# A seam as a planned list: the last block of a feed-forward layer and the first projections of the attention behind it

## The chip, the cores and the metric

The kernel runs on one core of a Trainium2 chip. The metric is the device time of one execution in microseconds, the median of the runs. The core's engines work side by side, each through its own queue of instructions in a fixed order: TensorE (PE, matrix products), VectorE (DVE), ScalarE (ACT), GpSimd (POOL) and SyncE (SP, which here issues the DMA transfers). An instruction starts when the one ahead of it on its engine and the instructions of other engines on which it depends are done.

## The reference, cut to what matters

Two layers on x of 1024 rows (S) by 1024 columns (D). Layer 0 mixes by a gated recurrence, layer 1 by stick-breaking attention with 16 heads of 64, and a SwiGLU feed-forward with an inner width of 2816 follows each. An RMS norm stands ahead of every sub-layer, a residual add behind it. The change lies at the seam between the feed-forward of layer 0 and the attention of layer 1:

```python
def swiglu_ffn(x, w_in, w_out):
    gu = jnp.einsum("bsd,df->bsf", x, w_in)
    h = jax.nn.silu(gu[..., :D_FF]) * gu[..., D_FF:]
    return jnp.einsum("bsf,fd->bsd", h, w_out)
...
    qkv = jnp.einsum("bsd,de->bse", x, w_qkv).reshape(bsz, seq, 3, N_HEADS, HEAD_DIM)
    ...
        z = jnp.einsum("bhqd,bhkd->bhqk", qb, kb).astype(jnp.float32) * scale
```

## The kernel before, in words

**Layout.** Activations lie transposed, columns on the 128 partitions: `h[d][n]` is part d (0 to 7) of the residual stream, half n (0 or 1, 512 rows). Every product is done in three passes (`mm3`, L545 to L547: high by high, low by high, high by low), so each operand exists as a rounded high part and the rest: for a part of the normed stream `xh` (ScalarE, L625) and `xl` (VectorE, L626), which the views name vh, vl or xg by the storage they use; for weights "hi" on ScalarE and "lo" on VectorE.

**The last block of the feed-forward.** The output product (p_ps) runs in 13 visits, each a pair of output parts d and d + 4 over a range of inner blocks. A visit makes seven products by combined weights instead of eight (`ORDER` is 0, 1, 2, 3, 4, 6, 5). Products that share a `BANK` add onto each other in PSUM; products 0, 2, 3 and 4 are first copied to SBUF by ScalarE (ta, tb; L1466) and products add to or subtract from `h` on VectorE ("post", L1468, L1470). A `Weights` object makes the combined weights: b (wbh, wbl), c (wch, wcl), d (wd). As soon as an `h[d][n]` is complete, `finished(d, n)` stores it (hd), makes xh and xl (`prep`) and adds its square to the sum of squares of half n (`squares`: ScalarE into acc, VectorE into rbc). In the generic loop this comes one product after the part was completed. The last visit, with parts 0 and 4, runs in this loop too, and a load and split of Q's first weights (raw, whi, wlo) is put between its products.

**The start of the attention.** A loop written out by hand takes the 8 parts (k = 0 to 7) of Q half 0, Q half 1, K half 0, K half 1 (qk_ps), and between them the steps of the row factors (`stats_steps`: sums L611, root, spread L592) and the splits of the next weights (`later`). Behind each group its result is scaled by the row factors (t, L1878), split (qh L1882, ql L1886), and SP moves it into per-head tiles (q, kh, kl; L1901; four moves for a half of Q, eight for a half of K). Loads of further weights (raw, L526) stand on the same queue, each where its group of the program calls for it.

**The plan.** All behind it is a `Plan`: tasks with an engine, an estimated cost, what they come after, and a rank. `emit` takes, again and again, the ready task that could begin first by these estimates (ties by rank), and writes it to its engine's queue. `attention_plan` holds the score chunks (z_ps, two banks in turn), their exponentials on ScalarE (F, L1953), the scans, the turned weights (wt_ps), the V products (av_ps) and the further projections.

Of the kernel before, what the change touches and what calls it, by code (L numbers as in the profile page):

```python
# [13 lines left out]
ALU = mybir.AluOpType  # L14
# [16 lines left out]
LATE = NB  # L31
FIRST = (ND, ND + 1, ND + 2, 0)


class Plan:
# [7 lines left out]
    def emit(self):  # L43
        end, free, table = {}, dict(self.free), {}
        todo, users = [], [[] for _ in self.tasks]
        for i, (_, _, _, after, _, _) in enumerate(self.tasks):
            after[:] = {a if isinstance(a, int) else a[0][a[1]] for a in after}
            todo.append(len(after))
            for a in after:
                users[a].append(i)  # L50
        ready = [i for i, n in enumerate(todo) if n == 0]
        while ready:
            best = None
            for i in ready:
                eng, us, _, after, rank, tab = self.tasks[i]
                begin = max([free[eng], *(end[a] + (0.0 if self.tasks[a][0] == eng else 0.15) for a in after)])
# [17 lines left out]
            fn()  # L74


# [113 lines left out]

def attention_plan(plan, fn):
    NP, LEAD = HEADS // 2, 8
# [24 lines left out]
    def weights(i, name, r, raw, use):  # L217
        ld = plan.add("dma", 4.8, fn["load", name], [raw], r - 4)
        h0 = plan.add("act", 0.5, fn["whi", name, 0], [ld, use], r - 2.5)
# [8 lines left out]
    is_kept = lambda q, n: q < NP - 2 + (n == 0)  # L228
    order = []
    for hx in range(2):  # L230
        moved[0, 1, 0, hx] = [plan.add(f"clock{hx}", 1.3 + 2.4 * hx, fn["wait", 0])]
    for i, (q, which, n) in enumerate(groups):
        s, wi = 24 * (q - 1) + 4 * (i % 6), 3 * q + which
        if i >= 4:
            if n == 0 and wi > 2:
                weights(wi, (q, which), s, wraw.get(wi - 3), wuse.get(wi - 2))
            p = None
            for k in range(ND):
                need = [p, pt.get(i - 2) if k == 0 else None]
                if wi > 2:  # L240
                    need.append(wlo[q, which][k // 4])
                p = plan.add("pe", 0.705, fn["proj", q, which, n, k], need, s + k / 2 + 0.5)
            proj[i] = wuse[wi] = p
        s += 4
        if i < 3:
            continue
        p = proj.get(i)
        if which < 2:
            order.append(i)
            was = order[-3] if len(order) > 2 else None  # L250
            pt[i] = plan.add("dve", 0.6, fn["t", q, which, n], [p, *moves.get(was, ())], s + 0.1)
            th = plan.add("act", 0.5, fn["qh", q, which, n], [pt[i], *moves.get(was, ())], s + 0.2)
# [7 lines left out]
        else:  # L260
            old = [(vadd, (q - 2, x)) for x in range(2)] if q > 1 else []
            pt[i] = plan.add("dve", 0.6, fn["t", q, which, n], [p, *old], s + 0.1)
            before = (dv, (q, n - 1) if n else (q - 1, 1)) if q or n else None
# [35 lines left out]
    tl, av, ring, banks, sums = {}, {}, [], [], {}  # L299
    stored = None  # L300
# [149 lines left out]
def trunk(  # L450
# [106 lines left out]
    class Mix:  # L557
# [8 lines left out]
        def load(self, i):  # L566
            self.raw[i] = load_raw(self.src[self.order[i]])
# [420 lines left out]
    def mix_out_ffn_in(h, mix, bias, layer, gnext, ob):  # L988
# [131 lines left out]
        with tc.manual_schedule(engines={E.PE, E.Activation, E.DVE, E.Pool}):  # L1120
# [359 lines left out]
            def finish(w):  # L1480
# [165 lines left out]
                end_plan(Plan(pe=0.0, act=0.9, dve=2.2, dma=0.0), Steps(acts), d0, d1, done).emit()  # L1646

            last_use = {p: max(u for u, (_, p0, p1) in enumerate(VISITS) if p0 <= p < p1) for p in range(NF // 2)}
            for s_, (kind, x) in enumerate(steps[:looped]):
# [18 lines left out]
                for k, i in enumerate(ORDER):  # L1668
# [4 lines left out]
                    part(banks[b], w, i, rhs[i], range(len(rhs[i])), onto=not new)  # L1673
                    if not final and kind == "v" and x == NV - 1:
                        if k == 0:
                            raw = load_raw(w_qkv[0])
                        elif k == 4:
                            qh = ring.four.tile([P, D], F32R, tag="w", name="whi")
                            nc.scalar.copy(qh, raw)
                        elif k == 5:  # L1680
                            ql = ring.four.tile([P, D], F32R, tag="w", name="wlo")
                            V.tensor_sub(ql, raw, f32(qh))
                            k3 = lambda t: t.rearrange("p (k c) -> p k c", k=ND)
                            wq0.append((k3(qh), k3(ql)))
                    if kind == "f":
                        post(x, i, banks[b])
                    else:
# [3 lines left out]
                        for dn in old:  # L1691
                            if final and x == NV - 3 and k >= L - 2:
# [90 lines left out]
            if not final:  # L1783
                for dn in done:
                    finished(*dn)
                del done[:]
        if final:
            with tc.manual_schedule(engines={E.PE, E.Activation, E.DVE, E.Pool, E.SP}):
                finish(nw)
        gs.close()  # L1790
# [7 lines left out]

    w_qkv, wq0 = attn_w_qkv, []
    mix_ffn(0, h, mix, V_BO, V_MIX + ND)  # L1800
# [16 lines left out]
    with ExitStack() as st:  # L1817
# [18 lines left out]
        TP, WH, WL, AV, OO, OH, OB = {}, {}, {}, {}, {}, {}, {}  # L1836
        W[0, 0] = wq0[0]

# [20 lines left out]

        def product(ps, name, k, n):  # L1860
            hi, lo = W[name] if name == (0, 0) else (k3(t) for t in W[name])
            mm3(ps, hi[:, k], lo[:, k], xh[k][n], xl[k][n], k == 0, k == ND - 1)

        def project(q, which, n, k):
            if k == 0:
                PS[q, which, n] = bank(psQ, "qk", n, "qk_ps")
            product(PS[q, which, n], (q, which), k, n)

# [186 lines left out]

        def stats_steps():
            for n in range(NH):
                stats(rbc[n], psO, f"o{n}", n)
                for _ in range(ND - (1 if n else 6)):
                    yield  # L2060
                broadcast_r(psO, f"o{n}", n)
                yield

        E = mybir.EngineType
        with tc.manual_schedule(engines={E.PE, E.Activation, E.DVE, E.Pool, E.SP}):
            sts, later = stats_steps(), []
            load((0, 1))
            load((0, 2))
            for i in range(4 * ND):
                if i >= 5:  # L2070
                    next(sts, None)
                g, k = divmod(i, ND)
                if k == 0:
                    if g:
                        was = (0, (g - 1) // 2, (g - 1) % 2)
                        scaled(*was)
                        q_hi(*was)
                        q_lo(*was)
                        for x in range(4 + 4 * was[1]):
                            move(*was, x)  # L2080
                    if g % 2 == 0:
                        name = (0, g // 2 + 1)
                        later += [
                            lambda a=name: w_hi(a, 0),
                            lambda a=name: (w_lo(a, 0), w_hi(a, 1)),
                            lambda a=name: w_lo(a, 1),
                        ]
                project(0, g // 2, g % 2, k)
                if i >= 5 and later:
                    later.pop(0)()  # L2090
# [64 lines left out]
```

## Time and profile before

| what | before |
|---|---|
| median of 3 runs | 2184.44 us (2180.5, 2184.44, 2184.8) |
| profiled execution, its own time | 2184.28 us |
| span of that execution | 2182.2 us |
| mean granted TensorE clock | 0.996 |
| TensorE busy | 2166.0 us (99%) |
| VectorE, ScalarE busy | 1705.2 us (78%), 1076.2 us (49%) |
| DMA | 274.62 MB, mean 126 GB/s |

Rows of a timeline give the start in microseconds from the span's start, the duration, the engine, the line, the operation, what it writes and reads and its shape, and in brackets the idle time of the engine just before with what ended it. TensorE's products overlap in part: what counts is the distance from one start to the next. Rows of the waits give the total, how often, and the longest. Rows of the windows give the stretch and its length, then the busy time of PE, PEld, DVE, ACT and POOL with their counts, then the granted clock of TensorE, the DMA share and GB/s.

### The profile page before, as it was taken

What the parts mean: (1) busy time and instruction counts of PE and PEld (TensorE: products, weight loads), DVE (VectorE), ACT (ScalarE), POOL (GpSimd) and SP (SyncE); (2) the same over time, 40 slices, a digit from 0 to 9 for tenths busy, and PEclk for the clock granted to TensorE, in tenths of its full rate; (3) what the DMA queues carried; (4) which work ended last, traced back from release to release, by engine and by line L of the source; (5) the groups of instructions that cost most, each with busy time, mean ns of one, the idle gap of its engine ahead of it and who ended that gap; (6) DMA issues with size and microseconds to landing.
All of it is one profiled execution on the core that took longest, in us unless ns stands there. A gap on an engine that the chain in (4) does not pass through costs nothing.

```text
span 2182.2 us, 27245 instructions
## 1 busy us (share of the span) xinstructions
PE 2166.0 (99%) x10066; PEld 1798.5 (82%) x10066; DVE 1705.2 (78%) x2431; ACT 1076.2 (49%) x1775; POOL 29.1 (1%) x38
## 2 busy tenths in 40 slices
PE   9999999999999999999999999999999999999998
PEld 7888888888888888877888888888888888888787
DVE  7978678677777887877888888877876777787887
ACT  5577445334444544644555555544543444454555
POOL 0000020000000000000000000001000000000000
PEclk9999999999999999999999999999999999999999
DMA  4111312244444854434333343442133444467452
GB/s 175 39 49 49 126 39 82 95 142 145 138 152 135 289 186 122 146 106 110 103 88 105 88 106 97 137 171 97 49 116 115 146 150 139 150 226 249 127 161 85
DMA packets 133317, 274.62 MB, mean 126 GB/s; under 512 B 15296, under 2 KB 23872, under 8 KB 133184
## 3 DMA queue, kind: packets, MB, share of 16 engines
q1 hardware_dynamic: 132768, 272.36, 39.5%
q8 instruction: 79, 1.29, 0.2%
q10 hardware_dynamic: 416, 0.52, 0.1%
q14 instruction: 54, 0.44, 0.1%
HBM read 176.88 MB, written 70.78 MB: 113 GB/s over the span
## 4 chain that ended last, share of the span: by engine, by line
PE 94%; DVE 3%; ACT 2%; issue 1%; DMA 0%; SPq 0%; DVEq 0%; ACTq 0%
PE p_ps L547 18%; PE p_ps L545 18%; PE p_ps L546 18%; PE qk_ps L545 4%; PE qk_ps L547 4%; PE qk_ps L546 4%; PE z_ps L1941 3%; PE av_ps L1989 3%; PE wt_ps L1972 3%; PE a_ps L546 3%; PE a_ps L547 3%; PE a_ps L545 3%; PE ob_ps L545 2%; PE ob_ps L546 2%; PE ob_ps L547 2%; PE g_ps L547 1%
## 5 line engine op out<-in xcount | busy, mean ns | idle before, releaser
L547 PE MATMUL p_ps<-vh,wal 128*128 128x512 f32 x524 | 204.2, 390 | 0.5 <-DVE wal L1061 0.4
L547 PE MATMUL p_ps<-vh,wcl 128*128 128x512 f32 x524 | 204.1, 390 | 0.5 <-DVE wcl L1080 0.5
L547 PE MATMUL p_ps<-vh,wbl 128*128 128x512 f32 x524 | 204.4, 390 | 0.0
L545 PE MATMUL p_ps<-vh,wch 128*128 128x512 f32 x524 | 204.1, 390 | 0.0
L545 PE MATMUL p_ps<-vh,wbh 128*128 128x512 f32 x524 | 204.1, 390 | 0.0
L546 PE MATMUL p_ps<-vl,wch 128*128 128x512 f32 x524 | 203.9, 389 | 0.0
L546 PE MATMUL p_ps<-vl,wbh 128*128 128x512 f32 x524 | 203.9, 389 | 0.0
L545 PE MATMUL p_ps<-vh,wah 128*128 128x512 f32 x524 | 203.9, 389 | 0.0
L546 PE MATMUL p_ps<-vl,wah 128*128 128x512 f32 x524 | 203.9, 389 | 0.0
L1953 ACT ACTIVATE F<-z_ps 128x512 f32<-128x512 f32 (+3 forms) x188 | 91.8, 489 | 181.9 <-PE z_ps L1941 181.8
L1066 ACT CAST wbh<-sb 128x1024 fp32r<-128x1024 f32 (+2 forms) x69 | 69.6, 1008 | 196.2 <-DVE sb L1050 196.1
L1960 DVE TENSOR_TENSOR_SCAN F<-F,unit 128x128 f32<-128x128 f32 (+3 forms) x128 | 105.0, 821 | 57.7 <-ACT F L1953 57.2
L545 PE MATMUL qk_ps<-vh,whi 128*128 128x512 f32 x264 | 121.1, 459 | 0.7 <-ACT vh L625 0.7
L547 PEld LDWEIGHTS p_ps<-vh,wal 128*128 128x128 f32 x524 | 98.4, 188 | 22.1 <-DVE wal L1061 1.8
L547 PEld LDWEIGHTS p_ps<-vh,wbl 128*128 128x128 f32 x524 | 98.3, 188 | 22.0 <-DVE wbl L1070 1.5
L547 PEld LDWEIGHTS p_ps<-vh,wcl 128*128 128x128 f32 x524 | 98.4, 188 | 21.8 <-DVE wcl L1080 1.3
L546 PEld LDWEIGHTS p_ps<-vl,wbh 128*128 128x128 f32 x524 | 98.4, 188 | 20.4
L545 PEld LDWEIGHTS p_ps<-vh,wch 128*128 128x128 f32 x524 | 98.4, 188 | 20.4
L546 PEld LDWEIGHTS p_ps<-vl,wah 128*128 128x128 f32 x524 | 98.4, 188 | 20.4
L546 PEld LDWEIGHTS p_ps<-vl,wch 128*128 128x128 f32 x524 | 98.4, 188 | 20.4
L545 PEld LDWEIGHTS p_ps<-vh,wah 128*128 128x128 f32 x524 | 98.4, 188 | 20.3
L545 PEld LDWEIGHTS p_ps<-vh,wbh 128*128 128x128 f32 x524 | 98.4, 188 | 20.2
(415 smaller groups left out, 5482.1 us busy)
## 6 DMA issues: line engine op xcount, KB each, us to landing
raw<-in_ffn_w_in SPq DMA_DIRECT2D x88, 512.0 KB, 3.7
vl<-pd SPq DMA_DIRECT2D x128, 256.0 KB, 3.7
pd<-U SPq DMA_DIRECT2D x90, 256.0 KB, 2.3
raw<-in_ffn_w_out SPq DMA_DIRECT2D x28, 512.0 KB, 4.2
raw<-in_attn_w_qkv SPq DMA_DIRECT2D x24, 512.0 KB, 3.9
kh<-qh SPq DMA_DIRECT2D x64, 128.0 KB, 2.3
kl<-ql SPq DMA_DIRECT2D x64, 128.0 KB, 2.3
acc<-pd SPq DMA_DIRECT2D x28, 256.0 KB, 2.6
```

The lines of the kernel that those rows point to most:

```text
L545: nc.tensor.matmul(ps, lhsT=wh, rhs=mh, start=first, stop=False, **kw)
L546: nc.tensor.matmul(ps, lhsT=wh, rhs=ml, start=False, stop=False, **kw)
L547: nc.tensor.matmul(ps, lhsT=wl, rhs=mh, start=False, stop=last, **kw)
L1066: nc.scalar.copy(self.full(self.wb), self.full(self.sb))
L1941: nc.tensor.matmul(ps[:, 0:n], lhsT=lhsT, rhs=rhs, start=i == 0, stop=i == 1)
L1953: nc.scalar.activation(F, Z.pop(c)[:, 0:n], AF.Sigmoid, scale=-SC)
L1960: V.tensor_tensor_scan(rev, rev, unit[:, NB - n :][:, ::-1], 0.0, op0=ALU.mult, op1=ALU.add)
L1972: nc.tensor.transpose(tp[:, c : c + P], F[:, (kb % 4) * P : (kb % 4 + 1) * P], ident)
L1989: nc.tensor.matmul(ps[:, c:], lhsT=VV[q][:, kb, hx], rhs=t.pop(u)[:, c:], start=kb == 4 * G and i == 0, stop=kb == 3 and i == 1,)
```

## The change

The last visit of layer 0's feed-forward leaves the generic loop (`looped` is one shorter) and becomes a plan of its own, `seam_plan`, with estimated costs and ranks: the steps of the weights b, c, d rank ahead of `finished`, and squares get a rank 20 higher. Its tasks include the loads of Q's, K's and V's first weights and the split of Q's. When it has been written out, the estimated times at which the parts, the sums of squares and the weights will be there go to `attention_plan` as `at`, and the times at which ScalarE, VectorE and SP are free become the start of the second plan.

The loop written by hand is gone. Its projections, the sums, roots, factors and spreads, the splits of weights and the moves are now tasks of `attention_plan`. The parts of every projection are taken in the order `KS` = 1, 5, 2, 6, 3, 7, 0, 4. K's first projections take their banks from another pool (psT). The row factor is computed by five small VectorE steps on the four columns instead of six; TensorE's products and the DMA transfers stay the same in number.

```diff
+KS = (1, 5, 2, 6, 3, 7, 0, 4)
...
+def seam_plan(plan, fn, d, left):
...
+    def finished(d, n, dep, r):
+        dma(2.4, ("store", d, n), [dep], r)
+        t = act(0.64, ("xh", d, n), [dep], r)
+        marks["x", d, n] = dve(0.66, ("xl", d, n), [t], r)
+        t = act(0.62, ("sq", d, n), [dep, added.get(n)], r + 20)
+        marks["acc", n] = added[n] = dve(0.6, ("sqadd", d, n), [t, added.get(n)], r + 20)
+
+    raw = dma(4.6, ("load", 0), [], 0)
+    raw1 = dma(4.6, ("load", 1), [], 1)
+    bl = dve(0.6, ("b_lo", 0), [], 0)
+    ch = act(0.65, ("c_hi", 0), [bl], 1)
+    cl = dve(0.7, ("c_lo", 0), [ch], 1)
+    raw2 = dma(4.6, ("load", 2), [cl], 3)
+    for k, t in enumerate(left):
+        finished(*t, None, 10 + k)
+    posts, src = {}, {}
+    dl = None
+    for k, i in enumerate((0, 1, 2, 3, 4, 6, 5)):
+        r = 1.4 * k
+        need = {2: [bl, src.get(0)], 3: [cl], 4: [src.get(2)], 6: [dl, src.get(3)], 5: [src.get(4)]}.get(i, [])
+        pe = plan.add("pe", 1.37, fn["prod", i], [pe, *need], r)
+        src[i] = pe
+        if i in (0, 2, 3, 4):
+            src[i] = act(0.5, ("copy", i), [pe, posts.get({3: 0, 4: 2}.get(i))], r)
+        after = {1: 0, 6: 2, 4: 3}.get(i)
+        posts[i] = dve(0.6, ("post", i), [src[i], posts.get(after)], r + 2)
+        if i in (1, 4, 6, 5):
+            finished(*{1: (d, 0), 4: (d + hk, 1), 6: (d, 1), 5: (d + hk, 0)}[i], posts[i], 14 + k)
+        if i == 1:
+            dh = act(0.4, ("d_hi", 0), [cl, pe], 4)
+            dl = dve(0.35, ("d_lo", 0), [dh], 4)
+        if i == 4:
+            qh = act(1.05, ("q_hi", 0), [raw, dl], 5)
+            marks[0, 0] = dve(1.2, ("q_lo", 0), [qh], 5)
...
-def attention_plan(plan, fn):
+def attention_plan(plan, fn, at):
...
+    known = {k: plan.add(("clock", k), max(t, 0.0), fn["wait", 0]) for k, t in at.items()}
+    for n in range(NH):
+        t = plan.add("pe", 0.95, fn["sums", n], [known["acc", n]], -17 + 2 * n)
+        t = plan.add("act", 0.25, fn["root", n], [t], -17 + 2 * n, "sqrt")
+        t = plan.add("dve", 1.0, fn["factor", n], [t], -17 + 2 * n)
+        t = plan.add("pe", 1.05, fn["spread", n], [t], -16 + 2 * n)
+        factors.append(plan.add("dve", 0.62, fn["rbc", n], [t], -16 + 2 * n))
...
+        for k in KS:
+            need = [p]
+            if p is None:
+                need.append(pt.get(i - 4 if i in (4, 5) else i - 2) if i > 3 else None)
+            if q == 0:
+                need += [known.get(("x", k, n))]
...
-            looped = len(steps) - (2 if final else 0)
+            looped = len(steps) - (2 if final else 1)
...
+                plan = Plan(pe=0.0, act=0.0, dve=0.8, dma=0.0)
+                marks = seam_plan(plan, Steps(acts), d, done)
+                end, free = plan.emit()
+                pre["free"] = {e: free[e] - free["pe"] for e in ("act", "dve", "dma")}
+                pre["at"] = {k: end[t] - free["pe"] for k, t in marks.items()}
...
-            plan = Plan(pe=0.0, dve=0.5, act=0.5, dma=1.3, clock0=0.0, clock1=0.0)
-            chunks, units = attention_plan(plan, Steps(acts))
+            plan = Plan(pe=0.0, **pre["free"])
+            chunks, units = attention_plan(plan, Steps(acts), pre["at"])
```

**ScalarE at the start of the last visit.** vh5_2, vh6_3 and vh5_3 are xh of three finished parts (from h7_0, h3_1, h7_1), acc are squares, wbh and wch the weights b and c, ta and tb copies of products out of their banks (p0_ps_7369 before and p0_ps_7362 now is the last visit's bank 0). Before:

```order
L1466 COPY tb_1909<-p0_ps_7248 128x512
L625 ACTIVATE vh5_3_2512<-h7_1_1886,vc_80 128x512
L621 ACTIVATE acc1_1888<-h7_1_1886 128x512
L1066 CAST wbh_7349<-sb_7315 128x2x256
L625 ACTIVATE vh6_3_2520<-h3_1_1878,vc_80 128x512
L621 ACTIVATE acc1_1888<-h3_1_1878 128x512
L1466 COPY ta_1908<-p0_ps_7369 128x512
L625 ACTIVATE vh5_2_2510<-h7_0_1885,vc_80 128x512
L621 ACTIVATE acc0_1887<-h7_0_1885 128x512
L1075 CAST wch_7385<-s1_7316 128x256
```

And now:

```order
L1519 COPY tb_1909<-p0_ps_7248 128x512
L1119 CAST wbh_7344<-sb_7315 128x2x256
L1744 ACTIVATE vh5_2_2510<-h7_0_1885,vc_80 128x512
L1744 ACTIVATE vh6_3_2520<-h3_1_1878,vc_80 128x512
L1744 ACTIVATE vh5_3_2512<-h7_1_1886,vc_80 128x512
L1741 COPY ta_1908<-p0_ps_7362 128x512
L1128 CAST wch_7389<-s1_7316 128x256
L1129 CAST wch_7389<-raw_7223 128x256
L1748 ACTIVATE acc0_1887<-h7_0_1885 128x512
L1748 ACTIVATE acc1_1888<-h3_1_1878 128x512
L1741 COPY tb_1909<-p0_ps_7362 128x512
```

The three xh stand together ahead of the visit's first copy (ta), the squares behind it; before, two xh and their squares stood ahead of the copy, and vh5_2 with its square behind it.

**VectorE at the same place.** The h lines are the adds into the residual parts, vl are the xl steps, rbc the sums of squares, wbl the low part of the weights b. Before:

```order
L1468 TENSOR_TENSOR h3_1_1878<-h3_1_1878,p3_ps_7303 128x512
L626 SCALAR_TENSOR_TENSOR vl5_3_2513<-h7_1_1886,vc_80,vh5_3_2512 128x512
L622 TENSOR_TENSOR rbc1_84<-rbc1_84,acc1_1888 128x512
L1053 TENSOR_TENSOR s4_7317<-sb_7315,raw_7188 128x256
L1470 TENSOR_TENSOR h7_0_1885<-p0_ps_7248,h7_0_1885 128x512
L626 SCALAR_TENSOR_TENSOR vl6_3_2521<-h3_1_1878,vc_80,vh6_3_2520 128x512
L622 TENSOR_TENSOR rbc1_84<-rbc1_84,acc1_1888 128x512
L1070 TENSOR_TENSOR wbl_7367<-sb_7315,wbh_7349 128x2x256
L1470 TENSOR_TENSOR h0_0_1871<-ta_1908,h0_0_1871 128x512
L626 SCALAR_TENSOR_TENSOR vl5_2_2511<-h7_0_1885,vc_80,vh5_2_2510 128x512
```

And now:

```order
L1521 TENSOR_TENSOR h3_1_1878<-h3_1_1878,p3_ps_7303 128x512
L1106 TENSOR_TENSOR s4_7317<-sb_7315,raw_7188 128x256
L1123 TENSOR_TENSOR wbl_7373<-sb_7315,wbh_7344 128x2x256
L1523 TENSOR_TENSOR h7_0_1885<-p0_ps_7248,h7_0_1885 128x512
L1745 SCALAR_TENSOR_TENSOR vl5_2_2511<-h7_0_1885,vc_80,vh5_2_2510 128x512
L1745 SCALAR_TENSOR_TENSOR vl6_3_2521<-h3_1_1878,vc_80,vh6_3_2520 128x512
L1717 TENSOR_TENSOR h0_0_1871<-h0_0_1871,ta_1908 128x512
L1133 TENSOR_TENSOR wcl_7400<-s1_7316,wch_7389 128x256
L1134 TENSOR_TENSOR wcl_7400<-raw_7223,wch_7389 128x256
L1717 TENSOR_TENSOR h0_0_1871<-h0_0_1871,p1_ps_7377 128x512
L1745 SCALAR_TENSOR_TENSOR vl5_3_2513<-h7_1_1886,vc_80,vh5_3_2512 128x512
```

wbl has moved from behind two vl steps, two sums and the add into h7_0 to a place ahead of all of these.

**SP at the moves of Q and K.** raw are weight loads of the attention, q, kh and kl the per-head tiles. Before:

```order
L1901 DMA q_7595<-qh1_7634 64x512
L1901 DMA q_7595<-ql1_7636 64x512
L1901 DMA q_7596<-qh1_7634 64x512
L1901 DMA q_7596<-ql1_7636 64x512
L1901 DMA kh_7679<-qh0_7675 64x512 x2
L1901 DMA kl_7681<-ql0_7677 64x512 x2
L1901 DMA kh_7680<-qh0_7675 64x512 x2
L1901 DMA kl_7682<-ql0_7677 64x512 x2
L526 DMA raw_7727<-in_attn_w_qkv 128x1024
L526 DMA raw_7732<-in_attn_w_qkv 128x1024
L1901 DMA kh_7679<-qh1_7725 64x512 x2
L1901 DMA kl_7681<-ql1_7734 64x512 x2
```

And now:

```order
L1995 DMA q_7646<-qh1_7660 64x512
L1995 DMA q_7645<-ql1_7665 64x512
L1995 DMA q_7646<-ql1_7665 64x512
L1995 DMA kh_7693<-qh0_7686 64x512 x2
L1995 DMA kl_7695<-ql0_7691 64x512 x2
L1995 DMA kh_7694<-qh0_7686 64x512 x2
L1995 DMA kl_7696<-ql0_7691 64x512 x2
L1995 DMA kh_7693<-qh1_7737 64x512 x2
L1995 DMA kl_7695<-ql1_7748 64x512 x2
L1995 DMA kh_7694<-qh1_7737 64x512 x2
L1995 DMA kl_7696<-ql1_7748 64x512 x2
L579 DMA raw_7786<-in_attn_w_qkv 128x1024
```

The two loads that stood between the halves of K's moves now come behind all of them; the loads that TensorE's next weights need have moved ahead of Q's moves.

More of the change, by code (lines that the diff above doesn't have):

```diff
@@ L1 @@
+from collections import defaultdict
 from contextlib import ExitStack
@@ L43, in emit @@
     def emit(self):
[L44 removed]
+        end, free, table = {}, defaultdict(float, self.free), {}
         todo, users = [], [[] for _ in self.tasks]
@@ L74, in emit @@
             fn()
+        return end, free
 class Steps:
@@ L217, in weights @@
     def weights(i, name, r, raw, use):
-        ld = plan.add("dma", 4.8, fn["load", name], [raw], r - 4)
+        ld = known.get(name) or plan.add("dma", 4.8, fn["load", name], [raw], r - 4)
         h0 = plan.add("act", 0.5, fn["whi", name, 0], [ld, use], r - 2.5)
@@ L250, in attention_plan @@
             was = order[-3] if len(order) > 2 else None
-            pt[i] = plan.add("dve", 0.6, fn["t", q, which, n], [p, *moves.get(was, ())], s + 0.1)
+            pt[i] = plan.add("dve", 0.6, fn["t", q, which, n], [p, turned_by, *moves.get(was, ())], s + 0.1)
             th = plan.add("act", 0.5, fn["qh", q, which, n], [pt[i], *moves.get(was, ())], s + 0.2)
@@ L1673, in mix_out_ffn_in @@
                     part(banks[b], w, i, rhs[i], range(len(rhs[i])), onto=not new)
[L1674 to L1684, printed above, removed]
                     if kind == "f":
@@ L1782, in mix_out_ffn_in @@
                         open_last()
[L1783 to L1789, printed above, removed]
+        with tc.manual_schedule(engines={E.PE, E.Activation, E.DVE, E.Pool, E.SP}):
+            (finish if final else seam)(nw)
         gs.close()
@@ L2054, in trunk, with column_sums @@
         }
[L2056 to L2062, printed above, removed]
+        def column_sums(n):
+            ST[n] = ps = bank(psO, "o", n, "st_ps")
+            for i in range(4):
+                nc.tensor.matmul(ps[:, i : i + 1], lhsT=rbc[n][:, i * P : (i + 1) * P], rhs=ones, start=True, stop=True)
@@ L2064, in trunk, with spread_out @@
+        def spread_out(n):
+            ST[n] = ps = bank(psO, "o", n, "rb_ps")
+            spread(ps, n)
+        ST = {}
+        acts |= {
+            "sums": column_sums,
+            "root": root,
+            "factor": factor,
+            "spread": spread_out,
+            "rbc": lambda n: V.tensor_copy(rbc[n], ST[n]),
+        }
+        for i in (1, 2):
+            raws[0, i] = pre["raw"][i]
         E = mybir.EngineType
         with tc.manual_schedule(engines={E.PE, E.Activation, E.DVE, E.Pool, E.SP}):
-            sts, later = stats_steps(), []
@@ L2067, in trunk @@
[L2067 to L2090, printed above, removed]
```

108 lines of the change are left out of this document (81 added, 27 removed).

## The prediction

> **What bounds the kernel now.** I read the page's busy times first, then TensorE's waits, then TensorE's timeline at each wait.
>
> ```profile
> PE 2166.0 (99%) x10066; PEld 1798.5 (82%) x10066; DVE 1705.2 (78%) x2431; ACT 1076.2 (49%) x1775; POOL 29.1 (1%) x38
> ```
>
> ```profile
> PE z_ps L1941 <- DMA kl<-ql: 2.5, 2, 2.0
> ...
> PE a_ps L611 <- DVE rbc L734: 0.8, 1, 0.8
> ...
> PE wt_ps L1972 <- DVE tl L1981: 0.6, 1, 0.6
> ```
>
> TensorE is the bound. The number of its matrix products does not change, so the change can gain only what TensorE loses between 940 and 1000 us, where the changed program runs: in waits and in slow clock. First the last feed-forward block:
>
> ```profile
> 942.80 0.39 PE L545 MATMUL p_ps<-vh,wbh 128*128 128x512 f32 x1
> 943.03 0.39 PE L546 MATMUL p_ps<-vl,wbh 128*128 128x512 f32 x1
> 943.46 0.50 PE L547 MATMUL p_ps<-vh,wbl 128*128 128x512 f32 x1
> 943.80 0.39 PE L545 MATMUL p_ps<-vh,wbh 128*128 128x512 f32 x1
> ...
> 944.72 0.40 PE L546 MATMUL p_ps<-vl,wch 128*128 128x512 f32 x1
> 945.66 0.50 PE L547 MATMUL p_ps<-vh,wcl 128*128 128x512 f32 x1 [0.54 <-DVE wcl L1080]
> ...
> 947.83 0.39 PE L547 MATMUL p_ps<-vh,wbl 128*128 128x512 f32 x1
> 948.65 0.50 PE L545 MATMUL p_ps<-vh,wd 128*128 128x512 f32 x1 [0.43 <-ACT ta L1466]
> ...
> 951.51 0.39 PE L547 MATMUL p_ps<-vh,wcl 128*128 128x512 f32 x1
> ...
> 954.13 0.39 PE L547 MATMUL qk_ps<-xg,wlo 128*128 128x512 f32 x1
> 955.17 0.50 PE L545 MATMUL qk_ps<-vh,whi 128*128 128x512 f32 x1 [0.65 <-ACT vh L625]
> 956.34 0.50 PE L546 MATMUL qk_ps<-vl,whi 128*128 128x512 f32 x1 [0.67 <-DVE vl L626]
> ...
> 988.93 0.39 PE L547 MATMUL qk_ps<-vh,wlo 128*128 128x512 f32 x1
> 991.33 0.45 PE L1941 MATMUL z_ps<-kh,q 128*128 128x128 f32 x1 [2.01 <-DMA kl<-ql]
> 992.28 0.45 PE L1941 MATMUL z_ps<-kl,q 128*128 128x128 f32 x1 [0.51 <-DMA kl<-ql]
> ```
>
> Undisturbed, starts are 0.23 us apart (942.80 to 943.03); behind a wait the next step is 0.34 (943.46 to 943.80), 0.11 more. Against that the steps into wbl, wcl, wd, vh and vl are too long by 0.20, 0.71, 0.59, 0.81 and 0.94, and four of them (vh runs straight into the next wait) cost 0.11 again: 0.31 + 0.82 + 0.70 + 0.81 + 1.05 = 3.69 us. The scores' two steps are 2.40 for 0.23 and 0.95 for some 0.06 (a quarter of the columns): 2.17 + 0.89 = 3.06.
>
> ```profile
> 36.00:40.00 4.00, 3.42 (x19) 2.99 (x20) 2.53 (x16) 0.20 (x1) 0.00 (x0) 1.00 0.00 0
> ...
> 943.00:950.00 7.00, 5.98 (x24) 3.93 (x23) 6.44 (x12) 4.98 (x10) 0.00 (x0) 1.00 0.60 202
> ...
> 955.00:960.00 5.00, 4.17 (x15) 3.26 (x16) 2.81 (x11) 3.06 (x6) 0.72 (x4) 0.72 0.14 52
> 960.00:970.00 10.00, 10.00 (x46) 8.62 (x45) 4.34 (x12) 0.92 (x3) 0.00 (x0) 0.80 0.06 14
> ...
> 990.00:1000.00 10.00, 8.16 (x29) 6.78 (x30) 4.08 (x7) 1.95 (x5) 0.00 (x0) 0.66 0.57 152
> ```
>
> Then the clock (the column before the DMA share). Between 955 and 970 the grant was short by 0.28 x 5 + 0.20 x 10 = 3.4 us, which is 6.8 us at half speed; between 990 and 1000 by 0.34 x 10 = 3.4, of which about 0.5 lay in the wait: 2.9. The first follows the waits of 0.65 + 0.67 = 1.32 us, the second that of 2.01. The waits at 943 to 950 (0.20, 0.54, 0.43) and the 0.78 at 36 to 40 were followed by none. So in this trace the clock halves after some 1.3 us idle close together and not after 0.8. All in all 3.69 + 3.06 + 3.4 + 2.9 = 13.0 us can go.
>
> **The last block.** The waits at wbl, wcl and wd arise because VectorE and ScalarE work off the finished columns first (the vl step, then the sum of squares) and the next weights behind them. The plan puts wbl before the h add, wcl before vl, and the squares behind the weights:
>
> ```profile
> 940.85 0.69 DVE L1470 TENSOR_TENSOR h<-p_ps,h 128x512 f32<-128x512 f32 x1
> ...
> 942.72 0.69 DVE L1070 TENSOR_TENSOR wbl<-sb,wbh 128x512 fp32r<-128x512 f32 x1
> ```
>
> ```profile
> 941.64 0.59 ACT L1466 COPY ta<-p_ps 128x512 f32<-128x512 f32 x1 [0.37 <-PE p_ps L547]
> 942.12 0.73 ACT L625 ACTIVATE vh<-h,vc 128x512 fp32r<-128x512 f32 x1
> 942.75 0.62 ACT L621 ACTIVATE acc<-h 128x512 f32<-128x512 f32 x1
> ...
> 954.39 0.72 ACT L625 ACTIVATE vh<-h,vc 128x512 fp32r<-128x512 f32 x1
> ...
> 972.93 1.14 ACT L1852 CAST whi<-raw 128x512 fp32r<-128x512 f32 x2
> ...
> 983.89 1.28 ACT L1953 ACT_TABLE_LOAD   x1
> 985.18 0.55 ACT L1953 ACTIVATE F<-z_ps 128x128 f32<-128x128 f32 x2
> ```
>
> On VectorE a vl step (0.75) and a sum (0.69) are now behind wbl (0.69), and so is the add that ended at 941.54: wbl is done by 941, 2 us before TensorE wants it (943.03 + 0.23). The time so won passes on to wcl and wd, whose splits also stand further ahead, and I set all three waits to zero. What covers them is VectorE's slack alone; were wcl late again, that is 0.82.
>
> A wait is added. ScalarE's queue now has three products "xh" (vh5_2, vh6_3, vh5_3) ahead of the copy of product 0 out of its bank, and TensorE's product 2 adds onto that bank. The first xh waits for VectorE's add into h7_0, which stands behind wbl. Before, the add ended at 941.54; wbl takes the place of a vl and a sum ahead of it, but may itself wait for its tile, so I keep 941.54. Three xh at 0.63 (942.12 to 942.75) end at 943.43, the copy's 0.59 at 944.02. TensorE arrives at 942.80: a wait of 1.24, with 0.11 behind it 1.35 us. If the add is done 0.6 earlier it is 0.75; if it comes 0.35 later, 1.70. Queued behind the copy are the splits wch (0.4 each), which TensorE wants only two products later (2.7 us).
>
> **The first projections.** Parts are taken in the order in which they are finished: the last finished (vh2_3) was the fifth and is now the eighth, due 7 x 3 x 0.23 = 4.8 us behind the block's last product. Before, that product began at 951.51 and vh2_3 was done at 954.39 + 0.72 = 955.11, 3.6 later, so 1.2 us are to spare, of which the weights' pair of casts (1.14), now ahead of it on ScalarE in place of one square (0.62), takes 0.5. That removes vh and vl (1.86) and, with them, the idle that halved the clock (3.4). The last squares now stand behind those casts and delay the row factors; no TensorE step waits for these, since K's products use banks of another pool; only the scaling of Q does. I take zero, with an upper bound of 0.69, one scaling step.
>
> **K's moves and the scores.**
>
> ```profile
> 975.08 1.17 SPq L1901 DMA_DIRECT2D q<-ql  x1
> ...
> 978.46 1.10 SPq L1901 DMA_DIRECT2D kh<-qh  x2
> ...
> 983.46 1.09 SPq L526 DMA_DIRECT2D raw<-in_attn_w_qkv  x2
> 984.65 1.11 SPq L1901 DMA_DIRECT2D kh<-qh  x2
> 985.85 1.20 SPq L1901 DMA_DIRECT2D kl<-ql  x2
> ```
>
> ```profile
> kh<-qh SPq DMA_DIRECT2D x64, 128.0 KB, 2.3
> ```
>
> A move takes SP 0.55 to 0.60 us and lands 2.3 us after its issue. The second half of K was issued right behind two weight loads, and the kl pair of 985.85 landed only when the product of 991.33 could start, 5.4 us on. In the plan the loads go behind all sixteen K moves. The second kl of 985.85 is then 12th in an unbroken row from 978.46: 978.46 + 11 x 0.60 = 985.1, landing 987.4. The scores come three full steps (0.68) earlier behind K's last product than before: 988.93 + 0.23 - 0.68 = 988.5. So the 3.06 and the 2.9 of half clock go, with 1.1 us to spare; if it is used up, up to 1.0 comes back.
>
> A second wait is added there. The third chunk of scores needs the bank that the first exponential frees. From K's last scaling on, ScalarE's chain is as before (cast, table load 1.28, F), and before, the third chunk started as F ended (985.18 + half of 0.55 = 985.46). It now stands 0.68 earlier in TensorE's program: about 0.72 with the hand-over, 0.83 with 0.11 behind it; nothing if ScalarE's chain starts earlier, 1.9 if the two weight casts ahead of it (1.14) still run when K ends.
>
> By the Trainium skill, "ScalarE: Activation LUTs", section What ACT_TABLE_LOAD costs, a switch takes 1283 ns and then a drain of some 1380 ns. The row here shows 1.28 and the next ACTIVATE 1.29 behind the load's start, so no drain; by the page this wait would be 1.4 longer and the time about 2174.8, by the row it is the 2173.4 below.
>
> **Rest.** From 1010 us on the plan orders the same work with the same lead; I set its balance at zero, bounds 0.6 either way: one such wait as that of wt for tl, in the first fence of waits.
>
> Sum: 13.0 removed, 1.35 + 0.83 = 2.2 added, 10.9 (rounded up) gained. The profiled execution took 2184.28 us, 0.16 below the median of the three runs, so 2184.28 - 10.9 = 2173.4 us.
>
> **Rivals.**
> 1. *The clock halves once more, after the new wait.* The 1.24 us idle at product 2 lies between the 0.78 that did no harm and the 1.32 that did. One stretch costs 3.4: 2176.8. For: it is one idle piece near the higher value. Against: nothing else is idle near it, and if it falls across two of the gate's windows each sees less. By the Trainium skill, "TensorE: Matmul & The Clock Gate", Part 1, the clock drops only after a whole idle window of about 3.4 us, which would give this rival no chance at all; this trace speaks against that, since the clock fell after 1.32 us idle.
> 2. *K's moves land late all the same.* Their own sixteen transfers crowd as the loads did; the scores wait 3.06 and the clock halves (2.9): 2173.4 + 6.0 = 2179.4. Against: the first eight moves, without loads, came in time.
> 3. *Nothing gained.* The new waits and late weights take back what the plan removes: about 2184, no change. VectorE is 90% busy from 943 to 950, and its order is all that the plan has to give there.
> 4. *Slower: SP's unbroken row of moves.* Two loads stand ahead of Q's moves and sixteen K moves follow without a pause. If a move takes 1.17 us, as one did at 975.08, and lands after 5.4, K's first four land at 978.46 + 3 x 1.17 + 5.4 = 987.4, where the scores want them at 984.32 less three and three more steps, 982.95: 4.4 us. The twelfth lands at 978.46 + 11 x 1.17 + 5.4 = 996.7 for 988.5 + 4.4: 3.8 more. Both waits halve the clock, 6.8: 15.0 us, 2188.4, slower than before. It decides from about 1.0 us a move and 4.6 to landing (3.1 + 2.4 + 6.8 = 12.3 against the 10.9 gained). Against: pairs took 1.10 to 1.20 throughout, loads or not.
>
> ```profile
> 984.32 0.22 PE L1941 MATMUL z_ps<-kh,q 128*128 128x128 f32 x1
> ```
>
> **How the numbers follow.** Forecast 2173.4: 0.50. Rival 1, 2176.8: 0.27. Rival 2, 2179.4: 0.11. Rival 3, 2184: 0.05. Rival 4, 2188.4: 0.07. The forecast's own bounds are 2171.2 (neither new wait) and 2175.5. The first two cases hold 0.77, so the range must reach the third: 2171.2 to 2179.6, which leaves out 0.12. Faster by over 0.2% (4.4 us, about what a measurement of this kernel can tell from no change) are the first three: 0.88; within it the fourth, 0.05; slower the last, 0.07.
>
> **What would show it.** In the changed profile: no wait for wbl, wcl or wd; one wait of about 1.2 us at TensorE for the copy into ta, near 943; no wait for vh or vl near 955; the clock at 1.00 from 955 to 1000; the scores waiting for F by some 0.7 and for kl not at all; the kl moves landing 2 to 3 us after issue. Below 1.00 behind 943 means rival 1; a wait for kl of over 2 us means rival 2, with moves of over 1 us rival 4. A wait of more than a microsecond behind 1010 us would mean that I priced the rest wrongly.

## The result: 2173.94 us, 0.35% faster

The changed kernel takes 2173.94 us (median of 6 runs, 2173.11 to 2175.16); the kernel before, now with 6 runs, 2180.44 (2179.0 to 2184.8). The ratio is 0.9965 with a 95% interval of 0.9953 to 0.9978. The forecast was 2173.4. In later runs, side by side on one chip, the gap was smaller: 2173.97 (10 runs) against 2179.42 (18 runs), a ratio of 0.9976 (0.9967 to 0.9986), or 5.4 us.

TensorE's waits in the profile of the changed kernel:

```profile
PE p_ps L598 <- ACT ta L1741: 1.2, 1, 1.2
PE z_ps L2035 <- DMA kl<-ql: 1.0, 1, 1.0
PE a_ps L664 <- DVE rbc L787: 0.8, 1, 0.8
```

The waits for vh, vl, wcl and for ta at wd are gone, and so are the two waits for kl at K's second half (2.5 together). Two are new: one for ta, and one of 1.0 for kl at K's first half, where the kernel before did not wait. The windows of the same trace, with the clock again in front of the DMA share:

```profile
943.00:950.00 7.00, 5.81 (x26) 4.49 (x25) 6.72 (x12) 6.73 (x13) 0.00 (x0) 1.00 0.68 228
950.00:955.00 5.00, 5.00 (x23) 4.14 (x23) 4.56 (x8) 3.63 (x6) 0.00 (x0) 1.00 0.38 109
955.00:960.00 5.00, 5.00 (x23) 4.13 (x22) 4.75 (x8) 2.11 (x4) 0.00 (x0) 1.00 0.43 164
960.00:970.00 10.00, 10.00 (x61) 8.85 (x60) 6.41 (x18) 3.99 (x7) 0.72 (x4) 1.00 0.32 117
970.00:980.00 10.00, 9.02 (x42) 7.31 (x41) 4.89 (x8) 4.20 (x7) 0.00 (x0) 1.00 0.78 179
```

TensorE is busy without a gap from 950 to 970, and the clock is 1.00 throughout (the rows up to 1010 show 1.00 too). Its timeline at the two new waits:

```profile
943.10 0.39 PE L600 MATMUL p_ps<-vh,wal 128*128 128x512 f32 x1
944.68 0.50 PE L598 MATMUL p_ps<-vh,wbh 128*128 128x512 f32 x1 [1.19 <-ACT ta L1741]
945.02 0.39 PE L599 MATMUL p_ps<-vl,wbh 128*128 128x512 f32 x1
...
977.76 0.30 PE L2035 MATMUL z_ps<-kh,q 128*128 128x128 f32 x1
979.03 0.30 PE L2035 MATMUL z_ps<-kl,q 128*128 128x128 f32 x1 [0.98 <-DMA kl<-ql]
```

The first costs 1.58 - 0.23 + 0.11 = 1.46 us, the second 1.27 - 0.06 = 1.21. How much the seam gave as a whole is read from the same product ahead of it and the same product far behind it, first in the trace of before, then in that of after:

```profile
926.09 0.39 PE L545 MATMUL p_ps<-vh,wah 128*128 128x512 f32 x1
...
1438.39 0.39 PE L547 MATMUL ob<-vh,wlo 128*128 128x512 f32 x1
```

```profile
926.72 0.39 PE L598 MATMUL p_ps<-vh,wah 128*128 128x512 f32 x1
...
1429.04 0.39 PE L600 MATMUL ob<-vh,wlo 128*128 128x512 f32 x1
```

That is 512.30 us before and 502.32 after, 10.0 less between these two executions. The medians differ by 6.5. The fifth experiment shows why.

### The profile page after: what moved, and what is told of

It is laid out like the page before. It is cut to its first block, busy times and chain, and to the rows that moved or that the text cites. A ratio compares the mean times of both kernels' runs of the same rounds, so it can differ in the third digit from the quotient of the medians.

```text
span 2173.0 us, 27239 instructions
## 1 busy us (share of the span) xinstructions
PE 2160.0 (99%) x10066; PEld 1793.4 (83%) x10066; DVE 1709.4 (79%) x2429; ACT 1086.4 (50%) x1775; POOL 29.1 (1%) x38
## 3 DMA queue, kind: packets, MB, share of 16 engines
q8 instruction: 79, 1.29, 0.2%
## 4 chain that ended last, share of the span: by engine, by line
PE 96%; DVE 2%; ACT 1%; issue 0%; DMA 0%; SPq 0%; POOL 0%; DVEq 0%; ACTq 0%; POOLq 0%
PE p_ps L600 18%; PE p_ps L598 18%; PE p_ps L599 18%; PE qk_ps L598 4%; PE qk_ps L600 4%; PE qk_ps L599 4%; PE z_ps L2035 3%; PE av_ps L2083 3%; PE wt_ps L2066 3%; PE a_ps L599 3%; PE a_ps L598 3%; PE a_ps L600 3%; PE ob_ps L599 2%; PE ob_ps L598 2%; PE ob_ps L600 2%; PE g_ps L599 1%
## 5 line engine op out<-in xcount | busy, mean ns | idle before, releaser
L2071 ACT CAST th<-wt_ps 128x512 fp32r<-128x512 f32 x192 | 92.2, 481 | 84.3 <-PE wt_ps L2066 77.1
L2075 DVE TENSOR_TENSOR tl<-wt_ps,th 128x512 fp32r<-128x512 f32 x192 | 104.7, 546 | 16.6 <-ACT th L2071 16.4
```

The source lines that it names most:

```text
L2071: nc.scalar.copy(WH[u][:, c:], TP[u][:, c:])
L2075: V.tensor_sub(WL[u][:, c:], TP.pop(u)[:, c:], f32(WH[u])[:, c:])
```

## Experiments

The median of the changed kernel was 2173.94 in its first runs and 2173.97 in 10 runs beside the seventh and eighth kernel. The kernel before, run beside all of them, has 60 runs more, from 2177.1 to 2183.1 with a median of 2179.2. Experiments 1 to 4, 5 to 8, and 9 and 10 ran on three different chips. Beside them the kernel before took 2179.1, 2179.4 and 2179.4, so a few tenths between experiments of different chips say little.

**1. The order of the parts undone.**

```diff
-KS = (1, 5, 2, 6, 3, 7, 0, 4)
+KS = (0, 1, 2, 3, 4, 5, 6, 7)
```

> The changed kernel with the parts of the projections taken in the order 0 to 7 again. Theory A (as predicted: the order of the parts is what removed the waits for vh and vl and the half clock behind them): waits for vh or vl of 1.7 us or more near 953 to 957 return, with a stretch of half clock, 2176 to 2179. Theory B (the plan of the last block alone finishes the parts early enough, the order is worth little): one wait of at most 0.3 us, clock 1.00, 2174 to 2174.5 against the 2173.9 of the changed kernel.

Measured: 2174.42 us (10 runs, 2173.94 to 2175.42). One wait is new in TensorE's timeline, and the clock stays at 1.00:

```profile
954.93 0.50 PE L599 MATMUL qk_ps<-vl,whi 128*128 128x512 f32 x1 [0.19 <-DVE vl L1745]
```

Theory B holds: taken alone, the order of the parts is worth 0.2 us of wait and some 0.5 in the time.

**2. The xh that waits, put behind the copy.**

```diff
     for k, t in enumerate(left):
-        finished(*t, None, 10 + k)
+        if t != (ND - 1, 0):
+            finished(*t, None, 10 + k)
...
+        if i == 0 and (ND - 1, 0) in left:
+            finished(ND - 1, 0, src[0], 10)
```

> The changed kernel, but xh of h7_0, the only one of the three that waits for an add, is put behind the copy of product 0. Theory A (the copy waits only because that xh stands ahead of it): the wait of 1.19 us for ta near 944 goes, 1.4 us with the slow step behind it, and what follows on the queues moves up with it: 2172.5, the wait for kl still about 1.0. Theory B (the moves of K hang on the row factors, which do not move up): the wait for kl grows by the 1.4 us that were won, to some 2.4, the time stays at 2173.9, and the clock may halve behind it, 2177.

The edit moves all of `finished` for h7_0: with xh also its store, xl and square.

Measured: 2172.21 us (6 runs, 2171.37 to 2173.19), 1.7 below the changed kernel. ScalarE's timeline now has the copy at 941.68 instead of 944.07, and TensorE runs into wbh without a wait; the later wait for kl stays:

```profile
941.68 0.59 ACT L1744 COPY ta<-p_ps 128x512 f32<-128x512 f32 x1 [0.35 <-PE p_ps L603]
942.16 0.41 ACT L1131 CAST wch<-s 128x256 fp32r<-128x256 f32 x1
```

```profile
942.78 0.39 PE L601 MATMUL p_ps<-vh,wbh 128*128 128x512 f32 x1
...
976.89 0.30 PE L2038 MATMUL z_ps<-kl,q 128*128 128x128 f32 x1 [0.97 <-DMA kl<-ql]
```

Theory A holds. The row factors and all that hangs on them moved up with TensorE, so the won time was not given back at kl.

**3. Finished parts and their squares ranked first.**

```diff
-        t = act(0.64, ("xh", d, n), [dep], r)
-        marks["x", d, n] = dve(0.66, ("xl", d, n), [t], r)
-        t = act(0.62, ("sq", d, n), [dep, added.get(n)], r + 20)
-        marks["acc", n] = added[n] = dve(0.6, ("sqadd", d, n), [t, added.get(n)], r + 20)
+        t = act(0.64, ("xh", d, n), [dep], r - 30)
+        marks["x", d, n] = dve(0.66, ("xl", d, n), [t], r - 30)
+        t = act(0.62, ("sq", d, n), [t, added.get(n)], r - 30)
+        marks["acc", n] = added[n] = dve(0.6, ("sqadd", d, n), [t, added.get(n)], r - 30)
```

> The changed kernel with xh, xl, square and sum of every finished part ranked ahead of the weights, as the loop before had them. Theory A (the rank of the squares is what the change buys in the last block): the copy of product 0 comes 0.6 to 1.2 us later, waits for wbl and wd of 0.4 to 0.5 return, 2 us in all; if the clock halves after about 1.3 us idle close together, 3.4 more: 2179; if it needs a whole idle window, 2176. Theory B on K's moves (the row factors are late because the squares are last): with squares first the wait for kl of 1.0 goes, 1.2 less in each case.

Measured: 2176.66 us (10 runs, 2175.39 to 2177.32), 2.7 above the changed kernel. TensorE's timeline:

```profile
944.78 0.50 PE L598 MATMUL p_ps<-vh,wbh 128*128 128x512 f32 x1 [1.78 <-ACT ta L1741]
945.96 0.50 PE L600 MATMUL p_ps<-vh,wbl 128*128 128x512 f32 x1 [0.45 <-DVE wbl L1123]
...
980.15 0.30 PE L2035 MATMUL z_ps<-kl,q 128*128 128x128 f32 x1 [0.80 <-DMA kl<-ql]
```

Theory A holds for the rank: against TensorE the copy is 0.6 later (1.78 idle for 1.19) and wbl waits, though no wait for wd came. In this execution the clock is 1.00 behind 1.78 + 0.45 us of idle, so my reading of the clock (halved after some 1.3 us close together) is not a rule. Theory B on K's moves falls: with the squares first, the wait for kl is still 0.80. The last sum of squares is complete at 958.75 here, 2.4 us earlier than in the changed kernel, but TensorE's product of the sums, on which the second row factor hangs, starts at 965.52 (964.12 in the changed kernel) without waiting for anything. The factors come when their turn in TensorE's queue comes; whether earlier factors would bring kl sooner no run shows.

**4. Loads back between the halves of K's moves.**

```diff
-        ld = known.get(name) or plan.add("dma", 4.8, fn["load", name], [raw], r - 4)
+        mid = (first, "ql") if i in (4, 5) else None
+        ld = known.get(name) or plan.add("dma", 4.8, fn["load", name], [raw, mid], r - 4)
...
+            if (q, which, n) == (0, 1, 0):
+                first["ql"] = tl
```

> The changed kernel with the two loads of the next weights put back between the halves of K's moves. Theory A (the loads between were what made the second half of K late): the scores wait 2 to 3 us for kl of the second half near 986, the clock halves, 3 + 3 us: 2179 to 2181. Theory B (the second half was late for another reason, its own sixteen moves or its late scaling): no wait beyond the 1.0 that is there already, 2173.9.

Measured: 2178.05 us (10 runs, 2176.02 to 2180.05), 4.1 above the changed kernel. SP's queue, TensorE and the clock:

```profile
978.86 1.07 SPq L582 DMA_DIRECT2D raw<-in_attn_w_qkv  x2
980.03 1.10 SPq L1998 DMA_DIRECT2D kh<-qh  x2
```

```profile
986.49 0.30 PE L2038 MATMUL z_ps<-kh,q 128*128 128x128 f32 x1 [2.05 <-DMA kh<-qh]
987.57 0.44 PE L2038 MATMUL z_ps<-kl,q 128*128 128x128 f32 x1 [0.78 <-DMA kl<-ql]
```

```profile
980.00:990.00 10.00, 7.17 (x28) 5.72 (x28) 4.87 (x7) 1.65 (x5) 0.00 (x0) 0.87 0.93 263
990.00:1000.00 10.00, 10.00 (x50) 8.23 (x49) 6.88 (x9) 5.18 (x11) 0.00 (x0) 0.95 0.00 0
```

Theory A holds: the second half of K is late because loads stand ahead of it; its first move was issued at 980.03 and TensorE could start only at 986.49. It is the landing that is late and not the issue: in the changed kernel the same move was issued at 979.85, and there K's moves landed 2.2 to 2.4 us after issue, here up to 5.9. The time is lower than expected because the half clock took 0.13 x 10 + 0.05 x 10 = 1.8 us in the profiled execution and not 3.

**5. The kernel before, profiled again.** No edit.

> The kernel before, unchanged, profiled a second time. Theory A (the half clock behind a wait is fixed by how long TensorE idles): the same waits as in the first profile, 0.65 + 0.67 near 956 and 2.0 + 0.5 near 991, and both stretches of half clock, 2184. Theory B (it depends on where the gate's windows lie against the waits, which differs from run to run): the same waits, but one stretch or both missing or shorter, 2177 to 2181, as the other runs of this kernel suggest.

Measured: 2179.22 us. TensorE's waits and the clock in this second execution:

```profile
955.37 0.51 PE L545 MATMUL qk_ps<-vh,whi 128*128 128x512 f32 x1 [0.61 <-ACT vh L625]
956.54 0.50 PE L546 MATMUL qk_ps<-vl,whi 128*128 128x512 f32 x1 [0.66 <-DVE vl L626]
989.21 0.30 PE L1941 MATMUL z_ps<-kh,q 128*128 128x128 f32 x1 [1.26 <-DMA kl<-ql]
990.18 0.30 PE L1941 MATMUL z_ps<-kl,q 128*128 128x128 f32 x1 [0.67 <-DMA kl<-ql]
```

```profile
955.00:960.00 5.00, 3.97 (x16) 2.96 (x17) 3.37 (x11) 3.36 (x6) 0.72 (x4) 0.80 0.14 52
960.00:970.00 10.00, 10.00 (x55) 8.68 (x54) 4.49 (x12) 0.82 (x2) 0.00 (x0) 0.93 0.18 43
...
990.00:1000.00 10.00, 9.82 (x51) 8.29 (x52) 7.75 (x12) 4.94 (x11) 0.00 (x0) 1.00 0.37 117
```

Theory A falls. The same places wait, but the clock takes 0.20 x 5 + 0.07 x 10 = 1.7 us in all, against 6.3 in the profile on which the forecast rests, and the waits for kl are 0.6 shorter. 4.6 + 0.6 are about the 5.1 between 2184.28 and 2179.22. The 60 runs agree: with a mean granted clock of 0.997 the kernel before takes 2182.3 (median of 6), with 0.998 2179.4 (30), with 0.999 2178.8 (24).

Theory B holds, and its reason can be read from the times at which the granted clock changed, which each trace records: 957.16, 963.99, 991.30 and 998.12 in the first profile, 957.98 and 961.39 in this one, 987.49 and 990.91 in experiment 4. Within one execution they lie 3.41 us or a multiple of it apart (6.83, 27.31 and 6.83 in the first). So in these traces the clock changes only at the ends of periods of 3.41 us, and the periods lie differently against the program in each execution. In the first profile the period that ended at 991.30 held 1.97 us of idle time. In the second, counted on from 957.98, a period ended at 988.70 in the middle of the wait: the idle time was split into 0.74 and 1.18, and the clock stayed at 1.00.

**6 and 7. Q's second moves behind K's first.** The sixth run is the changed kernel itself, as the reference. The seventh has this edit:

```diff
+                turn_of = [(first, 3)] if (q, which, n) == (0, 0, 1) else []
-                m = plan.add("dma", 2.4, fn["move", q, which, n, x], [src, *old], s + 0.3 + x / 100)
+                m = plan.add("dma", 2.4, fn["move", q, which, n, x], [src, *old, *turn_of], s + 0.3 + x / 100)
+                if (q, which, n) == (0, 1, 0):
+                    first[x] = m
```

> The changed kernel, unchanged, as the reference for the two that follow on the same chip: 2173 to 2175, the waits 1.2 for ta and 1.0 for kl again, no half clock.

> The changed kernel with the four moves of Q's second half put behind the eight moves of K's first half. Theory A (kl is late because these moves stand ahead of it on SP's queue): the wait for kl of 1.0 goes, 1.2 with the slow step, and the third chunk of scores then waits for F by 0.2 to 0.7, as I had predicted in its place: 0.5 to 1.0 less than the changed kernel. Theory B (kl is late because the row factors and so the scaled halves are late): kl still waits by 0.7 or more, no gain. Theory C (K's second half, which needs the buffers that Q's second half leaves, becomes late): a new wait of 1 us or more for kl or kh of the second half, slower than the changed kernel.

Measured: 2173.97 us for the changed kernel (10 runs, 2173.09 to 2175.38; kl waits 0.67 in its profile) and 2173.3 with the edit (9 runs, 2173.02 to 2175.1). First SP's queue and the critical chain's row in the changed kernel's first profile, then SP and TensorE with the edit:

```profile
972.11 1.23 SPq L1995 DMA_DIRECT2D q<-qh  x2
973.44 1.19 SPq L1995 DMA_DIRECT2D q<-ql  x2
974.73 1.18 SPq L1995 DMA_DIRECT2D kh<-qh  x2
976.00 1.18 SPq L1995 DMA_DIRECT2D kl<-ql  x2
```

```profile
976.59 2.31 DMA kl<-ql
```

```profile
972.80 1.10 SPq L1998 DMA_DIRECT2D kh<-qh  x2
974.00 1.19 SPq L1998 DMA_DIRECT2D kl<-ql  x2
```

```profile
977.24 0.28 PE L2038 MATMUL z_ps<-kl,q 128*128 128x128 f32 x1
...
978.78 0.39 PE L603 MATMUL qk_ps<-vh,wlo 128*128 128x512 f32 x1
979.25 0.45 PE L2038 MATMUL z_ps<-kh,q 128*128 128x384 f32 x1
```

Theory A holds: with K's moves ahead, kl is issued 2.0 us earlier (1.4 against TensorE, which itself is 0.6 earlier in this execution) and TensorE no longer waits for it. Now the third chunk (128x384) starts 0.47 behind its forerunner, 0.24 more than a normal step: the wait for F that I had forecast. The gain, 0.7, is what was expected less that wait, but it is about the spread of the runs; the waits, not the times, carry the verdict.

**8. All three.** The edits of 2 and 7, and an early load of F's table:

```diff
+        if n == 1:
+            plan.add("act", 1.5, fn["warm", 0], [t], -20)
...
+            "warm": lambda _: nc.scalar.activation(tiny[:, 60:61], tiny[:, 63:64], AF.Sigmoid, scale=1.0),
```

> Three edits at once: xh of h7_0 behind the copy, Q's second moves behind K's first, and the table of F loaded early by a dummy activation on one column behind the second root. If the three waits (ta 1.46 with its slow step, kl 1.2, F 0.2 to 0.7) are independent: all gone, 2.7 less than the changed kernel, about 2171.2, and the span within a microsecond of what the products alone take there. If the early table load delays the casts of q on ScalarE, kl waits by up to 1.3 again and the gain is 1.4 only.

Measured: 2171.32 us (5 runs, 2171.05 to 2172.61), 2.65 below the changed kernel on the same chip, and faster than both kernels. TensorE's timeline shows no wait from 940 to 1030. The gains add up to the 2.7 expected: the three waits are independent.

**9. Both orders undone.** The edits of 1 and 3 together.

> The changed kernel with both the rank of the finished parts and the order of the parts undone (the edits of the third and the first experiment together). Theory A (the rank of the finished parts and the order of the parts cover each other, so each alone looks worth little): a wait for vl or vh of 0.6 to 1.0 us returns near 956, where the first experiment showed 0.2 and the third none, 1 us above the third, 2177.5 to 2178. Theory B (the waits for vh and vl went for another reason, such as the scoring of all steps in one plan): no wait over 0.3 there, 2176.7 as the third.

Measured: 2177.97 us (10 runs, 2176.9 to 2179.36), 1.3 above the third. TensorE's timeline:

```profile
956.80 0.50 PE L599 MATMUL qk_ps<-vl,whi 128*128 128x512 f32 x1 [0.73 <-DVE vl L1745]
```

Theory A holds. The rank of the finished parts and the order of the parts each cover the same wait; only with both undone it comes back, by 0.73 of the 1.32 us that the kernel before waited. One rival is left: experiments 1, 3 and 9 also wait 1.2 to 1.8 us for ta, time in which VectorE and ScalarE get ahead. How much of the wait for vh and vl that covers is not shown; with the order kept, none returns when the wait for ta is gone (experiments 2 and 8).

**10. The early table without the moves.** The edits of 2 and of the table alone.

> The changed kernel with xh of h7_0 behind the copy and the table of F loaded early, but Q's second moves left ahead of K's first. Theory A (the table is not what the scores wait for as long as kl is late): the wait for kl of 0.7 to 1.0 stays, the time is that of the second experiment, 2172.2. Theory B (the table load ahead of K's casts counts as well): 0.3 or more below it.

Measured: 2171.93 us (5 runs, 2171.77 to 2172.44), 0.3 below the second experiment, which ran on another chip; kl waits only 0.36 here. The wait for kl was 0.98 and 0.67 in two profiles of the changed kernel, 0.97 in experiment 2 and 0.36 here, all with the same order of moves, so 0.3 cannot be put down to the table: inconclusive.

## Why the prediction was right, and where not

**The time.** 2173.94 against 2173.4, and the direction, hold. The size of the gain does not: 10.9 was forecast, and measured were 10.0 between the two profiles, 6.5 between the medians and 5.4 side by side. The step that failed is "0.16 below the median of the three runs": I took that execution as a fair picture of before. Its half clock took 3.4 + 2.9 us, that of the second profile 1.7, and of the 66 timed runs of before only two were as slow (2184.44 and 2184.8). The changed kernel showed none in two profiles, so its end time, worked out without half clock, came out right while the distance from before did not. Part of the hit is luck: a wait that I missed (1.21, below) and one that I expected and that did not come (0.83) nearly cancel. By the waits and the clock 13.0 went and 1.46 + 1.21 came, 10.4 in all; the 0.4 to the 10.0 measured lies within the 0.6 that I had left for the rest.

**The last block.** The waits for wbl, wcl and wd went. The added wait was forecast at 1.24 us from TensorE's arrival (944.02 - 942.80 is 1.22), 1.35 with the slow step, and measured 1.35 and 1.46. The 1.19 of the view counts from the modelled end of the product before, 0.16 later; the prediction set its 1.24 beside the idle times 0.78 and 1.32, which are counted in that way. The course is the one forecast; VectorE and ScalarE in the changed kernel:

```profile
940.88 0.69 DVE L1123 TENSOR_TENSOR wbl<-sb,wbh 128x512 fp32r<-128x512 f32 x1 [0.58 <-PE p_ps L599]
941.49 0.68 DVE L1523 TENSOR_TENSOR h<-p_ps,h 128x512 f32<-128x512 f32 x1
```

```profile
942.21 1.95 ACT L1744 ACTIVATE vh<-h,vc 128x512 fp32r<-128x512 f32 x3 [2.19 <-DVE h L1523]
944.07 0.56 ACT L1741 COPY ta<-p_ps 128x512 f32<-128x512 f32 x1
```

wbl did wait for its tile (0.58), and so the add ended at 942.17, 0.6 later than I had set it; the copy ended at 944.63. TensorE came as much later (943.33), because it was 0.6 us behind before the seam began (926.72 against 926.09), which is why the wait itself kept its size. Experiment 2 shows that the wait hung on the xh of h7_0: there the two other xh and even a square stand ahead of the copy, and TensorE does not wait.

**The first projections.** "That removes vh and vl" is right in the result, but the order of the parts, to which I gave the credit, is half of the cause: without it a wait of 0.19 is left (experiment 1), without the rank none (experiment 3), and only without both 0.73 (experiment 9).

**K's moves and the scores.** The wait at the second half of K went, for the reason given (experiment 4). But the first half of K was late, which I had put at "zero" beyond Q's scaling: "no TensorE step waits for these" (the row factors) is the step that failed. The chain of waits of the changed kernel runs from the sums through the row factors, the scaling and splits of Q and SP's moves to kl. Q's second moves, which wait for the factors, stood in the queue when K's first half was ready, and kl of 976.00 stood behind them in an unbroken row (experiment 7). That cost 1.21. The prediction had read K's moves and the scores in the times of before. But the scores came 6.6 us earlier (984.32, now 977.76), K's first move 3.7 (978.46, now 974.73), and Q's first move not at all (968.14, now 968.33). As the scores' first chunk was late, F was no longer late for the third, so the 0.83 of that wait was replaced, not added; experiment 7 brings it back at 0.24. The table load behaves as in before; ScalarE's timeline of the changed kernel has the next step 1.29 behind its start, without a drain:

```profile
978.70 1.28 ACT L2047 ACT_TABLE_LOAD   x1
979.99 0.55 ACT L2047 ACTIVATE F<-z_ps 128x128 f32<-128x128 f32 x2
```

**The rivals.** The half clock after the new wait did not come: the 16 runs of the changed kernel lie between 2173.09 and 2175.38, with a mean clock of 0.999 or 1.0. The 1.19 us of idle lay within one period of the clock (942.29 to 945.70), which was without work for 1.47 us, less than any of the four that end in a drop (last section). The row of moves did not slow: K's pairs took 1.18 to 1.24 us and landed 2.2 to 2.4 after issue, so rival 4 had nothing to stand on. The "1.10 to 1.20 throughout" that I set against it was read too narrowly: in before pairs took up to 1.25, and the one of 987.09, behind the loads, 1.98.

## What to carry to other kernels

Profile the kernel before more than once when its runs spread by more than a stall is worth: what one execution loses to the clock may be near the worst case, and belongs into the sum as a range. When a plan moves work ahead of a copy that the bound engine waits for, look whether one of the moved steps waits for something itself, since everything behind it on that engine inherits the wait. When several orders each remove a wait, undo them together before giving one of them the credit.

## What I had not expected of the hardware

The clock's answer to idle time was not the same for the same waits. It took 3.4 us behind 1.32 idle near 956 in one execution of before and 1.7 behind 1.27 in another; nothing behind 1.93 near 990 in that second one, but 1.8 behind 2.83 in experiment 4 and 3.4 behind 2.52 in the first; and nothing behind 1.78 + 0.45 within 3 us in the third experiment. By the Trainium skill, "TensorE: Matmul & The Clock Gate", Part 1, the clock drops after a whole idle window of about 3.4 us. The length agrees with the periods of 3.41 us that these traces show, but here the clock dropped with far less idle.

Counted by these periods, the cases sort. I laid the periods over TensorE's timeline in all twelve profiles, from 10 us on and without the end, and counted 0.23 us of work for a product of 512 columns, less in proportion for fewer. In the four periods that end in a drop, TensorE was without work for 3.16, 2.14, 2.12 and 1.87 us; in no other period at full clock for more than 1.80. In the third experiment the wait of 1.78 crossed the end of a period, and the fullest one had 1.68. The idle time of the views sorts less well, since it leaves out the 0.16 us by which the modelled ends run on: 1.27 in a period was followed by a drop, 1.52 in another was not. Four drops make this a rule of these traces and no more, and why the two of the first profile lasted 6.83 us and the others 3.41 is left open.
